# A rounded bias-table product, joined value products and a row factor moved behind a projection, in a hybrid RG-LRU and dilated-attention layer

## The chip, the cores and the metric

The kernel runs on one core of one Trainium2 chip, in one launch. The metric is the device time of the launch in microseconds; the median of three runs is given. The core has a matrix engine (TensorE, PE in the profile), a vector engine (VectorE, DVE), an activation engine (ScalarE, ACT), a general engine (GpSimd, POOL), and a queue engine (SyncE, SP) that only issues transfers. SP, ACT and POOL can each issue transfers between device memory and the on-chip memory. Each engine runs its own instructions in order and waits for the others by semaphores.

## What is computed

One layer of a bidirectional encoder on a sequence of 512 positions with 1024 channels, in 32-bit floats, as in this reference (cut):

```python
h = rms_norm(x, attn_norm_g)
xr, gate, q, k, v = split(h @ w_in)                 # 512 channels each
xr = centred_depthwise_conv(xr, conv_w, conv_b)
y_rnn = (rg_lru(xr, fwd) + rg_lru(xr, bwd)) * gelu(gate)
y_attn = dilated_attention(q, k, v, rel_bias)       # 8 heads of 64
mix = concat([rms_norm(y_rnn, norm_rnn_g), rms_norm(y_attn, norm_attn_g)])
x = x + mix @ w_out
h = rms_norm(x, mlp_norm_g)
x = x + square(relu(h @ w_up)) @ w_down             # 4096 hidden channels
return rms_norm(x, final_norm_g)
```

The attention of a head takes three windows of keys (strides 1, 4 and 16) with a bias that depends on the distance of key and query alone: `rel_bias` has 32 buckets by 8 heads. The kernel folds the three windows into one softmax over all 512 keys by adding to each score one number for the head and the distance: the bucket's bias, plus the logarithm of how many windows hold that distance, or -1e30 where none does. That table has 8 rows (heads) and 1024 columns (distances).

## The kernel before

Most tensors lie with channels on the 128 partitions and the 512 positions along the free dimension. Matrix products keep nearly full precision by splitting both operands into a rounded part (type fp32r, "hi") and the rounded remainder ("lo") and adding three rounded products (`mm3`, L222). Weights come from device memory as 128x1024 chunks on SP's queue (`emit_dma`, L182); each is split by ACT (`conv_hi`, L189) and DVE (`conv_lo`, L195) three chunks ahead of its use.

The order on each engine is the order of the program text: loops call small closures, and `plan` (L849) lists by hand which closure stands beside which step.

- The start (up to some 62 us) computes the recurrent input `pxr`, its convolution, the gates of the recurrence (`lru_gate`) and the value projection `pv`, 32 steps `n` of three rounded products (L592). In it `gate_weights` (L365) has POOL make the low parts of the gate weights, and `softplus_consts` (L120) has POOL make a few 128x8 constants, the last of them `chalf`.
- The bias table: ACT's queue loads `relt` (33 rows by 8: the 32 buckets and a row of ones) and two halves `oht` (33 rows by 512: a one-hot row for each bucket, and the logarithms) at L339 to L342. At step n = 18, `bias_prep` (L345) multiplies them on PE as plain 32-bit floats, DVE negates the result (`nbs`), and ACT's queue writes it to device memory (`nbd`). SP then loads, for each head, a 128x896 tile `tw` whose rows are shifted views of that row (`load_tw`).
- The gate projection and the first query and key projections follow (to some 100 us).
- The attention loop (L873) has 5 rounds `i` of 4 steps `u`. In round i, pair i of heads has its scores taken (`att_s`), reduced by DVE and exponentiated by ACT (`att_e`); pair i-1 has its probabilities transposed (`att_t`: PE to the two "et" buffers, and ACT copies them to `ett`). The value products of pair p (`att_av`, L742) run in two groups: key blocks 0 and 1 at step 2 of round p+1, key blocks 2 and 3 at step 0 of round p+2 (for the last pair after the loop). Each product writes 64 of the 128 rows of `pav`, two heads side by side. Beside each step run four "fillers": first the query and key projections of later pairs, then (`wo_thunks`, L780) the products of the recurrent half of `w_out`.
- The recurrent output `yrnn` (4 tiles) needs its RMS factor, one number for each position: squares (`sq_`, `add`), column sums on PE and the power on POOL (`rnn_cols`), then a tile with the factor along the free dimension on all partitions (`rnn_rows`: PE into an "et" buffer, and an ACT copy to `rr[0]`). DVE multiplies each `yrnn` tile by it (`rnn_scaled`, L506), and then the tile is split into hi (ACT, with the gain) and lo (DVE) for the products. The product of each of 8 output tiles is added to the residual `x1` by DVE (L792).
- After 210 us come the attention half of `w_out` and the feed-forward part, a dense stream of products to the end.

Of the kernel before, what the change touches and what calls it, by code (L numbers as in the profile page):

```python
# [12 lines left out]
FT = mybir.dt.float32  # L13
# [4 lines left out]
P = 128  # L18
# [22 lines left out]
for _n, _w in (("ag", 8), ("w0", 4), ("w1", 4), ("w2", 4), ("w3", 4), ("cb", 4),  # L41
# [2 lines left out]
    VEC[_n] = _o  # L44
    _o += _w
NVEC = _o


def bias_onehot():
    rel = np.arange(-(S - 1), S)  # L50
    m = np.zeros(rel.shape, np.int64)
    for window, dil in PATTERNS:
        half = window // (2 * dil)
        m += (rel % dil == 0) & (np.abs(rel) <= half * dil)
    nb = NBUCK // 2
    me = nb // 2
    n = np.abs(rel)
    nf = np.maximum(n, 1).astype(np.float32)
    large = me + (np.log(nf / np.float32(me)) / np.float32(math.log(MAXD / me))
                  * np.float32(nb - me)).astype(np.int32)  # L60
    large = np.minimum(large, nb - 1)
    bucket = np.where(rel > 0, nb, 0) + np.where(n < me, n, large)
    oh = np.zeros((NBUCK + 1, 2 * S), np.float32)
    oh[NBUCK, :] = NEG
    idx = np.arange(rel.size)
    keep = m > 0
    oh[bucket[keep], idx[keep]] = 1.0
    oh[NBUCK, idx[keep]] = np.log(m[keep].astype(np.float64)).astype(np.float32)
    return oh


@with_exitstack
def hybrid_kernel(ctx: ExitStack, tc, xw, xT, w_in, w_v, w_out, w_up, w_dn, gates, vecs, rel, onehot, fg, out):
# [261 lines left out]
            mm3(pxr[t], wk(t, k), hk(k), False, k == KD - 1)  # L335


    relt = consts.tile([NBUCK + 1, NH], FT, name="relt")
    nc.scalar.dma_start(relt, rel)  # L339
    oht = [work.tile([NBUCK + 1, S], FT, name="oht", tag="g", bufs=NG) for _ in range(2)]  # L340
    for i in range(2):
        nc.scalar.dma_start(oht[i], onehot[:, i * S:(i + 1) * S])  # L342
    nbd = dram.tile([NH, 2 * S], FT, name="nbd")

    def bias_prep():  # L345
        for i in range(2):
            pbz = ps_("pbias", "pj")
            nc.tensor.matmul(pbz[0:NH, :], lhsT=relt, rhs=oht[i], start=True, stop=True)
            nbs = g_("nbs", shape=(NH, S))
            nc.vector.tensor_scalar(nbs, pbz[0:NH, :], -1.0, None, op0=OP.mult)  # L350
            nc.scalar.dma_start(nbd[:, i * S:(i + 1) * S], nbs)
# [135 lines left out]
    def y_hi(k, y):  # L487
        ycat[k] = (g_("yh", FR), g_("yl", FR))
        act(ycat[k][0], y, AF.Copy, scale=vec("yg", k))

    def y_lo(k, y):
        hi, lo = ycat[k]
        stt(lo, y, vec("yg", k), f(hi), op0=OP.mult, op1=OP.subtract)
# [9 lines left out]
    def rnn_rows():  # L503
        rr[0] = row_tile(rc[0], "et")

    def rnn_scaled(*ts):  # L506
        for t in ts:
            nc.vector.tensor_tensor(yrnn[t], yrnn[t], rr[0], op=OP.mult)

    def rnn_split(*ts):  # L510
        for t in ts:
            y_hi(t, yrnn[t])
        for t in ts:
            y_lo(t, yrnn.pop(t))

    def proj_thunks(c, tag, done):
        o = {}

# [25 lines left out]
    def xmm(ks):  # L544
        for k in ks:
            mm3(pxr[3], wk(3, k), hk(k), k == 0, k == KD - 1)
# [11 lines left out]
    gate_weights(2)  # L558
    gate_weights(3)
    cneg, chalf = next(spc)  # L560
    xmm((1, 2, 3, 4))
    conv_b(0)
    conv_h(0)
# [28 lines left out]
    for n, (k, tt) in enumerate(steps):  # L592
        c = C_V + k // 2
        if k == 0:
            pv[tt] = ps_("pv", vtag[tt])
        hi, lo = splits[c]
        sl = slice((k % 2) * S, (k % 2 + 1) * S)
        tsl = slice(tt * P, (tt + 1) * P)
        mm3(pv[tt], (h_hi[:, k, tsl], h_lo[:, k, tsl]), (hi[:, sl], lo[:, sl]), k == 0, k == KD - 1)
        if n >= 16:  # L600
            feed(c, n % 8)
        if n in (8, 11, 14):
            conv_hi({8: 6, 11: 7, 14: 8}[n])
        if n in (9, 12, 15):
            conv_lo({9: 6, 12: 7, 15: 8}[n])
        if n >= GA and n < GA + 12 and (n - GA) % 3:
            t, m = (n - GA) // 3, 2 * ((n - GA) % 3 - 1)
            lru_gate(t, m)
            lru_gate(t, m + 1)
        if n == 0:  # L610
            conv_b(2)
        if n == 2:
            conv_b(3)
        if n == GA + 1:
            conv_h(2)
            conv_c(2)
        if n == GA + 2:
            conv_h(3)
            conv_c(3)
        lru_hooks(n)  # L620
        if n == 18:
            bias_prep()
            load_tw(0)
            load_tw(1)
# [155 lines left out]
    def wo_thunks(half, c2):  # L780
        c = C_WO + half * 4 + c2
        o = {}

        def mk(j, k):
            def run():
                if k == 0:
                    o["p"] = ps_("pwo", "pj")
                mm3(o["p"], wok(c, j, k), ycat[half * 4 + k], k == 0, k == 3)
                feed_q(c, 4 * j + k)
                if k == 3:  # L790
                    cc = 2 * c2 + j
                    nc.vector.tensor_tensor(x1[cc], x1[cc], o["p"], op=OP.add)  # L792
            return run
        return [mk(j, k) for j in range(2) for k in range(4)]

# [31 lines left out]
    def rnn_sq(t):  # L827
        y_sq(yrnn[t], 0)

    def scaled(t):  # L830
        return lambda: rnn_scaled(t)

    def hi(t):
        return lambda: y_hi(t, yrnn[t])

# [3 lines left out]
    def end(t):  # L839
        return lambda: rnn_end(t)  # L840

    def sq_(t):
        return lambda: rnn_sq(t)

    def add():
# [3 lines left out]
    plan = {(0, 0, 2): [sq_(0), add], (0, 0, 3): [end(1)],  # L849
            (0, 1, 1): [sq_(1)],  # L850
            (0, 2, 3): [add],
            (1, 0, 2): [end(2)], (1, 0, 4): [sq_(2)],
            (1, 1, 0): [add], (1, 1, 2): [end(3)], (1, 1, 4): [sq_(3)],
            (1, 2, 0): [add], (1, 2, 2): [rnn_cols], (1, 3, 1): [rnn_rows],
            (1, 3, 3): [scaled(0)], (1, 3, 4): [scaled(1), hi(0), hi(1)],
            (2, 1, 2): [lo(0), lo(1)], (2, 1, 3): [scaled(2), scaled(3), hi(2), hi(3)], (2, 2, 2): [lo(2), lo(3)]}
    for i in range(3):
        for key, (is_k, fn, e) in {(0, 2): (1, s_hi, 0), (0, 3): (1, s_hi, 1), (1, 0): (1, s_lo, 0), (1, 1): (1, s_lo, 1),
                                   (2, 2): (0, s_hi, 0), (2, 3): (0, s_hi, 1), (3, 0): (0, s_lo, 0), (3, 1): (0, s_lo, 1)}.items():
# [13 lines left out]
    for i in range(5):  # L873
        for u in range(4):
            if i < 4:
                att_s(i, u)
                if u == 0 and i < 3:
                    load_tw(2 * i + 2)
                if u == 2 and i < 3:
                    load_tw(2 * i + 3)  # L880
            if i >= 1:
                att_t(2 * i - 2, u)
                att_t(2 * i - 1, u)
            if i < 4:
                att_e(i, u)
            if u == 2 and i >= 1:
                att_av(i - 1, (0, 1))
            if u == 0 and i >= 1:
                att_z(i - 1)
            if u == 0 and i >= 2:  # L890
                att_av(i - 2, (2, 3))
            beside(i, u, 0)
            fill(1)
            beside(i, u, 1)
            fill(1)
            if u == 1 and i >= 1:
                att_r(i - 1)
            if u == 0 and i >= 2:
                att_y(i - 2)
            beside(i, u, 2)  # L900
            fill(1)
            beside(i, u, 3)
            fill(1)
            beside(i, u, 4)
# [25 lines left out]
    wo_b(0, 0)  # L930
    wo_b(0, 1)
    conv_hi(c + 3)
    att_av(3, (2, 3))
    att_y(3)
    wo_b(0, 2)
    for k in range(3):
# [353 lines left out]
```

## Time and profile before

| | us |
|---|---|
| runs (three) | 566.73, 566.97, 567.18; median 566.97 |
| profiled execution: its own time | 566.53 |
| profiled execution: span of the instructions | 564.8 |
| granted TensorE clock, mean over the span | 0.994 |
| busy: DVE, ACT, POOL | 388.7, 313.5, 51.9 |
| first bias product, first `nbs` | 53.3, 54.3 |
| attention loop, first and last step's transposes | 117.8, 198.5 |
| last matrix product starts | 555.3 |

"Span" is the time from the first to the last instruction of the profiled execution; its own time is longer by what lies around it. In the timeline view of the profile a row gives start and duration in us, engine, source line, operation, output <- inputs, the shape, how many instructions were merged (x8), and in brackets how long the engine had been idle and what ended that. A matrix product's duration includes its way through the array, and the next one starts earlier: the distance of two starts is what a product costs. A product of plain 32-bit floats shows as two rows.

### The profile page before, as it was taken

What the parts mean: (1) busy time and instruction counts of PE and PEld (TensorE: products, weight loads), DVE (VectorE), ACT (ScalarE), POOL (GpSimd) and SP (SyncE); (2) the same over time, 40 slices, a digit from 0 to 9 for tenths busy, and PEclk for the clock granted to TensorE, in tenths of its full rate; (3) what the DMA queues carried; (4) which work ended last, traced back from release to release, by engine and by line L of the source; (5) the groups of instructions that cost most, each with busy time, mean ns of one, the idle gap of its engine ahead of it and who ended that gap; (6) DMA issues with size and microseconds to landing.
All of it is one profiled execution on the core that took longest, in us unless ns stands there. A gap on an engine that the chain in (4) does not pass through costs nothing.

```text
span 564.8 us, 6888 instructions
## 1 busy us (share of the span) xinstructions
PE 554.5 (98%) x2520; PEld 445.0 (79%) x2520; DVE 388.7 (69%) x610; ACT 313.5 (56%) x510; POOL 51.9 (9%) x70
## 2 busy tenths in 40 slices
PE   9999999999999999999999999999999999999993
PEld 7887888677677678888888888888888888888782
DVE  6896499986774439453477778977233676896894
ACT  7669993686966434154463566553223243665654
POOL 3370000000000000000003033001000000131000
PEclk9999999999999999999999999999999999999997
DMA  7803434343351212242339799959623234699603
GB/s 262 297 12 113 169 113 149 113 131 113 111 187 38 74 38 75 75 149 75 104 109 287 171 268 275 266 164 258 186 84 104 77 110 98 194 252 262 163 1 149
DMA packets 25494, 82.97 MB, mean 147 GB/s; under 512 B 3106, under 2 KB 3234, under 8 KB 25460
## 3 DMA queue, kind: packets, MB, share of 16 engines
q1 hardware_dynamic: 19968, 64.50, 33.3%
q0 software_dynamic: 4608, 16.78, 15.5%
q10 hardware_dynamic: 884, 1.25, 0.7%
q8 instruction: 20, 0.33, 0.2%
q14 instruction: 14, 0.11, 0.1%
HBM read 78.81 MB, written 2.13 MB: 143 GB/s over the span
## 4 chain that ended last, share of the span: by engine, by line
PE 88%; DVE 6%; DMA 2%; ACT 2%; issue 1%; ACTq 0%; DVEq 0%
PE pu L224 10%; PE pu L223 10%; PE pu L225 10%; PE pd L224 6%; PE pd L223 6%; PE pd L225 6%; PE pqk L223 3%; PE pwo L223 3%; PE pav L749 3%; PE pqk L225 3%; PE pwo L225 3%; PE pwo L224 3%; PE pqk L224 3%; PE pt L716 2%; DMA wraw<-in_w_dn_dram 2%; DVE wlo L199 2%
## 5 line engine op out<-in xcount | busy, mean ns | idle before, releaser
L199 DVE TENSOR_TENSOR wlo<-wraw,whi 128x1024 fp32r<-128x1024 f32 x81 | 98.8, 1221 | 38.3 <-ACT whi L192 38.2
L192 ACT ACTIVATE whi<-wraw 128x1024 fp32r<-128x1024 f32 x81 | 85.4, 1055 | 41.1 <-PE pd L225 15.7
L223 PE MATMUL pu<-h2h,whi 128*128 128x512 f32 x256 | 100.5, 392 | 0.0
L225 PE MATMUL pu<-h2h,wlo 128*128 128x512 f32 x256 | 99.8, 390 | 0.0
L224 PE MATMUL pu<-h2l,whi 128*128 128x512 f32 x256 | 99.7, 390 | 0.0
L224 PE MATMUL pd<-wlo,ah 128*128 128x512 f32 x192 | 74.9, 390 | 0.1
L225 PE MATMUL pd<-whi,al 128*128 128x512 f32 x192 | 74.8, 389 | 0.0
L223 PE MATMUL pd<-whi,ah 128*128 128x512 f32 x192 | 74.8, 389 | 0.0
L1013 ACT ACTIVATE a<-pu 128x512 f32<-128x512 f32 x32 | 19.0, 597 | 97.6 <-PE pu L225 97.6
L1014 DVE TENSOR_TENSOR a<-a 128x512 f32<-128x512 f32 x32 | 22.1, 692 | 65.5 <-ACT a L1013 65.5
L225 PEld LDWEIGHTS pu<-h2h,wlo 128*128 128x128 f32 x256 | 48.1, 188 | 10.1
L223 PEld LDWEIGHTS pu<-h2h,whi 128*128 128x128 f32 x256 | 48.1, 188 | 9.8
L224 PEld LDWEIGHTS pu<-h2l,whi 128*128 128x128 f32 x256 | 48.1, 188 | 9.7
L224 PEld LDWEIGHTS pd<-wlo,ah 128*128 128x128 f32 x192 | 36.1, 188 | 7.9 <-DVE wlo L199 0.5
L223 PEld LDWEIGHTS pd<-whi,ah 128*128 128x128 f32 x192 | 36.1, 188 | 7.5
L225 PEld LDWEIGHTS pd<-whi,al 128*128 128x128 f32 x192 | 36.1, 188 | 7.4
L192 ACT ACTIVATE whi<-ts 128x1024 fp32r<-128x1024 f32 x24 | 25.5, 1061 | 24.2 <-PE pd L225 16.5
L199 DVE TENSOR_TENSOR wlo<-ts,whi 128x1024 fp32r<-128x1024 f32 x24 | 29.3, 1222 | 8.8 <-ACT whi L192 8.5
L205 POOL DMA_DIRECT2D ts<-in_w_dn_dram x16 | 16.9, 1175 | 106.5 <-DVE wlo L199 106.5
L223 PE MATMUL pqk<-h_hi,whi 128*128 128x512 f32 x64 | 26.5, 414 | 0.0
L223 PE MATMUL pwo<-yh,whi 128*128 128x512 f32 x64 | 26.3, 412 | 0.0
L718 ACT ACTIVATE ett<-pt 128x512 f32<-128x512 f32 x32 | 17.3, 590 | 15.8 <-PE pt L716 15.8
(210 smaller groups left out, 1031.6 us busy)
## 6 DMA issues: line engine op xcount, KB each, us to landing
wraw<-in_w_up_dram SPq DMA_DIRECT2D x32, 512.0 KB, 3.3
wraw<-in_w_dn_dram SPq DMA_DIRECT2D x24, 512.0 KB, 6.6
ts<-in_w_dn_dram POOLq DMA_DIRECT2D x24, 512.0 KB, 12.0
wraw<-in_w_in_dram SPq DMA_DIRECT2D x13, 512.0 KB, 3.3
wraw<-in_w_out_dram SPq DMA_DIRECT2D x8, 512.0 KB, 3.3
ts<-in_w_dn_dram SPq DMA_DIRECT2D x8, 512.0 KB, 5.3
tw<-in_w_dn_dram SPq DMA_DIRECT2D x8, 512.0 KB, 6.8
tw<-in_w_dn_dram POOLq DMA_DIRECT2D x8, 512.0 KB, 11.5
```

The costliest lines, as they stand in the source:

```text
L192: act(hi, raws[i], AF.Copy)
L199: nc.vector.tensor_tensor(lo, r, f(splits[i][0]), op=OP.subtract)
L205: nc.gpsimd.dma_start(r, wblock(c[0], nxt[1], c[2]), accum_op=OP.add)
L223: nc.tensor.matmul(o, lhsT=a[0], rhs=b[0], start=bool(first), stop=False)
L224: nc.tensor.matmul(o, lhsT=a[0], rhs=b[1], start=False, stop=False)
L225: nc.tensor.matmul(o, lhsT=a[1], rhs=b[0], start=False, stop=bool(last))
L716: nc.tensor.transpose(pt[:, qt * P:(qt + 1) * P], en[h][qt][:, jt * P:(jt + 1) * P], ident)
L718: act(t, pt, AF.Copy)
L749: nc.tensor.matmul(pav[p][a, :], lhsT=vs[:, jt, h * DH:(h + 1) * DH], rhs=et.pop((h, jt)), start=jt == 0, stop=jt == 3)
L1013: act(r, p, AF.Relu)
L1014: nc.vector.tensor_tensor(r, r, r, op=OP.mult)
```

## The change

It has three parts.

1. The bias table. `bias_rows` repeats the bucket rows on the host: buckets, buckets again, the row of logarithms, 31 zero rows, and that row again: 97 rows. `relt` becomes 97x128 (the 8 heads padded with zeros to 128 columns) and the halves of `oht` 97x512. They are loaded by POOL's queue, after `chalf`, in place of ACT's at the start. New `bias_round`, at steps n = 14 and n = 16, has DVE round them to fp32r: the second copy of the bucket rows gets the remainder of the table, and the last row gets the remainder of the logarithms (its factor is one). `bias_prep` then does one rounded product for each half.
2. The value products of a pair run in one group of eight at the later of the two places.
3. The row factor of the recurrent output is not multiplied into `yrnn`; it is multiplied into each of the 8 outputs of the recurrent projection, before the sum with `x1`. `rnn_scaled` and `rnn_split` go, and `plan` moves the squares, splits, column sums and row tile to other steps.

```diff
+NB3 = 3 * NBUCK + 1
...
-    return oh
+    return bias_rows(oh)
+
+
+def bias_rows(a):
+    b, last = a[:NBUCK], a[NBUCK:]
+    return np.concatenate([b, b, last, np.zeros((NBUCK - 1, a.shape[1]), np.float32), last], axis=0)
...
-    relt = consts.tile([NBUCK + 1, NH], FT, name="relt")
-    nc.scalar.dma_start(relt, rel)
-    oht = [work.tile([NBUCK + 1, S], FT, name="oht", tag="g", bufs=NG) for _ in range(2)]
-    for i in range(2):
-        nc.scalar.dma_start(oht[i], onehot[:, i * S:(i + 1) * S])
+    relt = consts.tile([NB3, P], FT, name="relt")
+    oht = [work.tile([NB3, S], FT, name="oht", tag="g", bufs=NG) for _ in range(2)]
     nbd = dram.tile([NH, 2 * S], FT, name="nbd")
+
+    ohr = []
+    relr = consts.tile([NB3, P], FR, name="relr")
+
+    def bias_round(i):
+        if i == 0:
+            r = slice(NBUCK, 2 * NBUCK)
+            nc.vector.tensor_copy(relr, relt)
+            nc.vector.tensor_tensor(relr[r], relt[r], f(relr)[r], op=OP.subtract)
+        t = work.tile([NB3, S], FR, name="ohr", tag="g", bufs=NG)
+        ohr.append(t)
+        r = slice(3 * NBUCK, NB3)
+        nc.vector.tensor_copy(t, oht[i])
+        nc.vector.tensor_tensor(t[r], oht[i][r], f(t)[r], op=OP.subtract)
 
     def bias_prep():
         for i in range(2):
             pbz = ps_("pbias", "pj")
-            nc.tensor.matmul(pbz[0:NH, :], lhsT=relt, rhs=oht[i], start=True, stop=True)
+            nc.tensor.matmul(pbz, lhsT=relr, rhs=ohr[i], start=True, stop=True)
...
     cneg, chalf = next(spc)
+    nc.gpsimd.dma_start(relt, rel)
+    for i in range(2):
+        nc.gpsimd.dma_start(oht[i], onehot[:, i * S:(i + 1) * S])
...
+        if n in (14, 16):
+            bias_round((n - 14) // 2)
         if n == 18:
             bias_prep()
...
-                    nc.vector.tensor_tensor(x1[cc], x1[cc], o["p"], op=OP.add)
+                    t = g_("wot")
+                    nc.vector.tensor_tensor(t, o["p"], rr[0], op=OP.mult)
+                    nc.vector.tensor_tensor(x1[cc], x1[cc], t, op=OP.add)
...
-            (1, 0, 2): [end(2)], (1, 0, 4): [sq_(2)],
-            (1, 1, 0): [add], (1, 1, 2): [end(3)], (1, 1, 4): [sq_(3)],
-            (1, 2, 0): [add], (1, 2, 2): [rnn_cols], (1, 3, 1): [rnn_rows],
-            (1, 3, 3): [scaled(0)], (1, 3, 4): [scaled(1), hi(0), hi(1)],
-            (2, 1, 2): [lo(0), lo(1)], (2, 1, 3): [scaled(2), scaled(3), hi(2), hi(3)], (2, 2, 2): [lo(2), lo(3)]}
+            (1, 0, 2): [end(2)],
+            (1, 1, 0): [sq_(2)], (1, 1, 2): [end(3)], (1, 1, 4): [add],
+            (1, 3, 0): [sq_(3)], (1, 3, 2): [hi(0)], (1, 3, 3): [add, hi(1)], (2, 0, 2): [rnn_cols],
+            (2, 0, 0): [lo(0), lo(1)], (2, 0, 4): [hi(2)],
+            (2, 1, 1): [rnn_rows], (2, 1, 2): [hi(3)], (2, 1, 4): [lo(2)], (2, 2, 3): [lo(3)]}
...
-            if u == 2 and i >= 1:
-                att_av(i - 1, (0, 1))
             if u == 0 and i >= 1:
                 att_z(i - 1)
             if u == 0 and i >= 2:
-                att_av(i - 2, (2, 3))
+                att_av(i - 2, range(4))
...
-    att_av(3, (2, 3))
+    att_av(3, range(4))
```

A key of `plan` is (round, step, place within the step).

## The prediction

> **What bounds the kernel now.** I read the page's busy table first, then who waits on TensorE (the waits view of PE), then the timeline of PE around each place that the change touches, and last DVE, ACT and POOL at the same moments.
>
> ```profile
> PE 554.5 (98%) x2520; PEld 445.0 (79%) x2520; DVE 388.7 (69%) x610; ACT 313.5 (56%) x510; POOL 51.9 (9%) x70
> PE pwarm L118 <- DVE epsb L109: 1.0, 1, 1.0
> 180.00:200.00 20.00, 20.00 (x110) 14.60 (x109) 8.84 (x15) 9.37 (x18) 0.00 (x0) 1.00 0.18 53
> ```
>
> PE is busy 98% of the span, and the only wait of PE in the waits view is 1.0 us before the first warm-up product. The third line (a stage: PE, PEld, DVE, ACT, POOL busy, clock, DMA share, GB/s) shows the attention stage: PE 20.00 of 20, clock 1.00, DVE not half busy. So PE sets the time, and an edit counts by what it takes from PE's stream or by the wait it puts into it. Busy is not the price, since matmuls overlap; the step from one start to the next is.
>
> ```profile
> 52.51 0.39 PE L223 MATMUL pv<-whi,h_hi 128*128 128x512 f32 x1
> 52.74 0.39 PE L224 MATMUL pv<-wlo,h_hi 128*128 128x512 f32 x1
> ...
> 53.28 1.88 PE L348 MATMUL pbias<-oht,relt 33*8 33x512 f32 x4
> 55.09 0.50 PE L223 MATMUL pv<-whi,h_hi 128*128 128x512 f32 x1
> 55.43 0.40 PE L224 MATMUL pv<-wlo,h_hi 128*128 128x512 f32 x1
> ...
> 122.31 1.03 PE L716 MATMUL pt<-ident,e 128*128 128x128 f32 x8
> 123.11 0.48 PE L223 MATMUL pqk<-h_hi,whi 128*128 128x512 f32 x1
> 123.42 0.40 PE L224 MATMUL pqk<-h_lo,whi 128*128 128x512 f32 x1
> ...
> 127.31 1.04 PE L716 MATMUL pt<-ident,e 128*128 128x128 f32 x8
> 128.27 1.94 PE L749 MATMUL pav<-ett,vs 128*64 128x512 f32 x8
> 130.14 0.50 PE L223 MATMUL pqk<-h_hi,whi 128*128 128x512 f32 x1
> 130.48 0.40 PE L224 MATMUL pqk<-h_lo,whi 128*128 128x512 f32 x1
> ```
>
> The pv rows are rounded (fp32r) products of 512 columns: one a 0.227 us. The two plain f32 bias products run as four passes (x4). An attention-value group (pav) holds four plain products, two jt by two heads, also two passes each: x8.
>
> **Part 1, the bias table.** From 53.28 to the second pv start after it (55.43) are 2.15 us; a pv product alone would have taken 0.23 of it, so the group costs 1.92. Afterwards it is two rounded products of 97 rows to 128 columns, the width of their neighbours: 2 x 0.227 = 0.45. Gain 1.47 us of PE. If the rounded product ran in two passes as the plain one does (0.43 each), it would be 0.2: I take one pass, since every f32r product in the page has one row.
>
> What it adds stands on DVE and POOL, and decides whether PE waits.
>
> ```profile
> 45.42 1.23 DVE L199 TENSOR_TENSOR wlo<-wraw,whi 128x1024 fp32r<-128x1024 f32 x1 [2.02 <-ACT whi L192]
> 48.68 1.23 DVE L199 TENSOR_TENSOR wlo<-wraw,whi 128x1024 fp32r<-128x1024 f32 x1 [2.03 <-ACT whi L192]
> 49.83 3.70 DVE L407 TENSOR_TENSOR ga<-ga,xc 128x512 f32<-128x512 f32 x6
> 54.34 0.68 DVE L350 TENSOR_SCALAR nbs<-pbias 8x512 f32<-8x512 f32 x1 [0.82 <-PE pbias L348]
> 39.85 0.71 POOL L145 TENSOR_SCALAR chalf<-sp 128x8 f32<-128x8 f32 x1
> ```
>
> bias_round(0) stands on DVE between the first two lines: table copy and difference (128 columns, some 0.2 us each, an estimate from the 0.36 of the 128x384 cast at L256), one 97x512 copy (0.43, the row of the 512-column copy L729) and a one-row difference (0.69, as any 512-column two-input row): 1.4 us in an idle 2.03, free. bias_round(1) stands behind four of the six L407 (0.60 apart): 49.83 + 2.41 = 52.24, then 0.36 + 0.69 and about 0.06 for the signal: 53.35. PE's second product wants it at 53.28 + 0.23 = 53.51. No wait, with 0.16 us to spare. lru_x(2), nbs and lru_x(3) behind it come 1.1 us later; the weight difference after them (59.98) had been idle for 2.84 us, so nothing beyond it moves.
>
> This holds if the rows have landed. Three issues leave ACT, where they hid beside a wait for weights (2.49 us idle before 19.62): worth nothing to PE. They stand on POOL behind chalf, which ends at 40.56; nothing of POOL's waits behind them until the rnn factor some 90 us later. Two POOL issues in a row start 0.55 to 0.92 us apart in the trace, so the halves are issued at about 41.2 to 41.5 and 41.8 to 42.4. If the first half lands at t, PE waits until t + 5.7 (0.36 + 0.69 copy and difference, 1.15 weight difference, 2.41 for L407, 0.36 + 0.69, signal 0.06) against 53.51: a landing up to 47.8 is free, then each us costs a us.
>
> ```profile
> ts<-in_w_dn_dram POOLq DMA_DIRECT2D x24, 512.0 KB, 12.0
> DMA to landing us min/median/max: 5.3/14.0/19.4
> q10 hardware_dynamic: 44, 0.07, 8.6%
> ```
>
> No plain load from POOL is in the trace: all 32 of its transfers add 512 KB into a tile (first two lines; the least, 5.3 us, is a lone one). Those packets are 4 KB and take 0.327 us, eight to each DMA engine: 2.6 us, so 2.7 us of a lone one is start and completion. A half of the table is 97 rows of 2 KB; on the ACT queue such a row took 0.084 us (the packet records of the old load). Over 16 engines it is 7 rows: 0.6 us, landing 3.3 us after issue, at 44.7; with the 5.3 of the nearest row, 46.7. Both are free. Upper bound: all 97 rows on one engine, 97 x 0.084 = 8.1, landing at 41.4 + 2.7 + 8.1 = 52.2, a wait of 4.4 us (on one and the same engine the second half would come at 60.3: 7.9 us); or the median of all, 12.0, at 53.4: 5.6. The third line (17 to 21 us: packets, MB, share) is one old load of 33 rows: 44 packets, 33 rows and 11 more, one for each engine: it went to 11 engines with three rows each, not to 16. I take 3.3 to 5.3, because the cost above the transfer is nearest to a lone POOL row.
>
> By the Trainium skill, DMA: Bandwidth & Descriptors, section "Why a DMA increments its semaphore by 16 and not by 1", a copy takes the largest number of engines up to 16 that divides its rows, which is 11 for 33 rows: the trace agrees. By that rule 97, a prime, would take one engine, and the sum would be a loss; the same section has an exception for some copies from GpSimd, with the rows rounded up over 16, and by that the sum stays. No run here yet shows which. [...]
>
> **Part 2, value products in one group.** From pt at 127.31 to the second pqk at 130.48 are 3.17 us; the same stretch without the group (122.31 to 123.42) is 1.11. A group costs 2.06: four pairs of passes 0.43 apart (1.72) and 0.34 of entering and leaving the 64-column products. A joined group is 8 x 0.43 + 0.34 = 3.78 against 4.12. The last pair's second group (200.87) stands alone and joins too, so four pairs gain 4 x 0.34 = 1.38 us. If the entry were paid anew inside, nothing: the three equal steps in each group speak against that. The transposed tiles wait a step longer for their reader; there are 48 buffers of that tag, and about 25 are taken between.
>
> **Part 3, the row factor.** PE's work is the same: column sums (0.90) and row tile (0.44) only move, the first from step (1,2) to (2,0), the second from (1,3) to (2,1). DVE loses four products at 138 to 151 us (0.68 each) and gains eight at 160 to 200 (0.69 each, before each sum). Cover: DVE is idle 8.1 and 11.2 us in the two stages 160 to 180 and 180 to 200, and 5.5 is asked. Queued behind each pwo sum are the next step's score reductions, which PE's next scores wait for; without cover, eight times up to 0.69. The shortest step without value products is 0.80 + 12 x 0.227 + 0.09 + 0.91 = 4.5 us; DVE's in it 1.3 (reductions) + 0.6 (half a weight difference) + 1.3 + about 0.7 = 3.9. It fits. One thing gets late: the row tile now goes into the "et" buffer that the first transposes of its step leave.
>
> ```profile
> 146.45 1.04 PE L716 MATMUL pt<-ident,e 128*128 128x128 f32 x8
> 147.38 1.06 ACT L718 ACTIVATE ett<-pt 128x512 f32<-128x512 f32 x2
> ```
>
> In the old place the row tile came 1.56 us after pt; here that is 148.01, while the first ett copy, behind a weight cast, ends at 147.97 and needs its signal. I put 0.1 us (0 to 0.5, the second copy).
>
> **Sum.** 1.47 + 1.38 - 0.1 = 2.75 us. The profiled execution took 566.53 us (span 564.8, and 1.7 around it): 563.8. The median of the runs is 0.44 above it, so 566.97 - 2.75 = 564.2. After 210 us every stage is PE's dense stream, so the gain passes through: 10 us of PE idle lie at the start and behind the last product, and neither is touched.
>
> **Rivals.** (a) The rows come late, slower than before. Place: PE's bias products. Price: a us for each us that the first half lands after 47.8; at a landing of 50.5 the gain is gone, from 51.7 on the kernel is slower. One engine: 564.2 + 4.4 = 568.6; 12.0 us: 569.8. For it: 33 rows took 11 engines, a divisor, and 97 has none up to 16 but 1; and every POOL transfer is between 5.3 and 19.4. Against: those moved 2.6 times the bytes, adding, with DMA engines up to 90% busy; here their share is 0.25. Chance 0.12. (b) Late by part of that, landing at 48 to 50.5: 564.5 to 567. POOL's small rows at 31 to 40 us take 0.7 instead of 0.2 beside busy DVE, which speaks for some delay. 0.10. (c) The attention stage gives a part back: steps without value products shrink from 6.6 to 4.5 us while ACT, 16.4 of 20 us busy at 140 to 160, has as much to do; three pairs losing up to 0.5 each: 565.7. Against: the time taken there comes back in the joined step (9.2 us). 0.09. (d) Rounded product in two passes, or entry paid again: 565.0 to 565.6. 0.03.
>
> **How the numbers follow.** Forecast 0.66 (563.7 to 564.6). I call 0.2%, 1.1 us, what can be told from no change: faster is under 565.8, slower over 568.1. Faster: forecast, nearly all of (c), (d), half of (b): 0.66 + 0.08 + 0.03 + 0.05 = 0.82, less 0.04 for what I don't see: 0.78. Same: rest of (b) and (c) and a little: 0.10. Slower 0.12. The range reaches from 563.6 through (c) to the end of (b), 566.8.
>
> **What would show it.** In the changed profile: two pbias rows 0.23 apart and no wait of PE for DVE ahead of them (wait there: rival a or b, with the landing of oht to match); four pav rows of x16, each 3.35 to the last start; the row tile 1.6 us behind its transposes; DVE idle still left between 160 and 200 us; one lag of 2.7 us from 210 to the end. Wrong it would be if PE shows any wait of more than 0.5 us.

## The result and the profile after

The changed kernel took 564.01 us (median of six executions, the fastest 563.5; five lie within 564.71), the kernel before 567.0 us in the same comparison: a ratio of 0.9947, 95% interval 0.9933 to 0.9961. Run again for the study it took 564.53 us against 566.88 us, ratio 0.9951 (0.9937 to 0.9965). One of the first six executions, the one that was profiled, took 1,984.56 us with its products 0.84 us apart, which no other execution did; the profile shown here is that of the second time (e0_after, 564.53 us, span 562.8 us).

First its busy table:

```profile
PE 552.2 (98%) x2518; PEld 445.5 (79%) x2518; DVE 394.7 (70%) x620; ACT 313.4 (56%) x510; POOL 54.0 (10%) x73
```

Then what PE waited for (us in total, times, longest):

```profile
PE pwarm L124 <- DVE epsb L115: 1.0, 1, 1.0
PE pd L230 <- DVE wlo L205: 0.7, 1, 0.7
```

And the stage 180 to 200 us (columns as in the prediction):

```profile
180.00:200.00 20.00, 20.00 (x109) 13.04 (x107) 9.91 (x15) 8.35 (x15) 0.00 (x0) 1.00 0.16 53
```

PE is still the bound. The wait of 0.7 us lies at 529 us, far from the change: a product starts 0.87 us later there than the usual distance of two products (0.227 us). The same product is late by 0.26 us in the kernel before, and by anything from nothing (e4_late_rows) to 0.72 us (e6_value_cols) in the other profiles. DVE has 10.1 us of idle time left in the last attention stage (11.2 before).

Then PE's timeline around the bias products, an attention step without value products, one with them, and the new place of the row tile:

```profile
53.29 0.39 PE L231 MATMUL pv<-whi,h_lo 128*128 128x512 f32 x1
53.52 0.79 PE L366 MATMUL pbias<-ohr,relr 97*128 97x512 f32 x2
54.15 0.40 PE L229 MATMUL pv<-whi,h_hi 128*128 128x512 f32 x1
...
130.80 1.04 PE L729 MATMUL pt<-ident,e 128*128 128x128 f32 x8
131.59 0.48 PE L229 MATMUL pqk<-h_hi,whi 128*128 128x512 f32 x1
...
135.34 1.04 PE L729 MATMUL pt<-ident,e 128*128 128x128 f32 x8
136.31 3.65 PE L762 MATMUL pav<-ett,vs 128*64 128x512 f32 x16
139.89 0.50 PE L229 MATMUL pqk<-h_hi,whi 128*128 128x512 f32 x1
...
145.94 0.40 PE L231 MATMUL pqk<-h_hi,wlo 128*128 128x512 f32 x1
146.27 0.62 PE L308 MATMUL prow<-ident,rcol 128*128 128x128 f32 x4
```

The bias group is two rows (x2) and 0.63 us long, from 53.52 to 54.15; the second of the two starts at 53.83. A joined value group is sixteen rows and 3.58 us long where two groups took 1.87 each; the transposes before it last 0.97 us to the next start, where those without a group last 0.79. The row tile follows the product before it by 0.33 us, 0.1 more than the distance of two products.

Last the rows of the table on their way. POOL's issues:

```profile
40.92 0.84 POOL L569 DMA_DIRECT2D relt<-in_rel_dram  x1
41.76 1.13 POOL L571 DMA_DIRECT2D oht<-in_onehot_dram  x2
```

The page's line for the transfer (KB each, us from issue to landing):

```profile
oht<-in_onehot_dram POOLq DMA_DIRECT2D x2, 194.0 KB, 2.9
```

And DVE:

```profile
47.44 0.43 DVE L360 CAST ohr<-oht 97x512 fp32r<-97x512 f32 x1
47.90 0.69 DVE L361 TENSOR_TENSOR ohr<-oht,ohr 1x512 fp32r<-1x512 f32 x1
48.99 1.23 DVE L205 TENSOR_TENSOR wlo<-wraw,whi 128x1024 fp32r<-128x1024 f32 x1 [0.40 <-ACT whi L198]
...
52.54 0.42 DVE L360 CAST ohr<-oht 97x512 fp32r<-97x512 f32 x1
53.00 0.69 DVE L361 TENSOR_TENSOR ohr<-oht,ohr 1x512 fp32r<-1x512 f32 x1
```

The first half landed at 41.76 + 2.9 = 44.7 us. Its rounding stands in an idle stretch of DVE. The second half's ends at 53.69, and PE's second bias product starts at 53.83, 0.147 us later and 0.316 us after the first. That product waits for DVE. In every run with the changed table it starts 0.146 or 0.147 us after this rounding ends, while its distance from the first product varies from 0.316 (here) to 0.44 us (e5_rows_act_queue); and the two products of e4_late_rows that wait for DVE for far longer start 0.146 us after the rounding too. Against the usual distance the wait is 0.09 us here; the waits view doesn't list it, since the products overlap.

The parts are worth a quarter of a per cent each, and single executions of the kernel before spread over 0.3% (566.32 to 568.13 us), so the parts are also read by lag: the start of the same product in two profiles, subtracted. The change of the lag from one landmark to the next belongs to the stage between them. (Start of the product in the profile, less that in the kernel before; us.)

| | last input product, 28.8 | last gate product, 50.9 | first gate projection, 64.1 | last projection product, 224.6 | last product, 555.3 |
|---|---|---|---|---|---|
| e0_after | +0.41 | +0.33 | -1.06 | -2.29 | -1.69 |
| e1_bias_alone | +0.34 | +0.22 | -1.13 | -1.26 | -1.22 |
| e2_value_alone | +0.42 | +0.06 | +0.06 | -0.37 | -0.14 |
| e3_row_alone | +0.13 | -0.23 | -0.23 | -0.13 | -0.11 |
| e6_value_cols | +0.55 | +0.19 | +0.19 | -1.17 | -0.68 |
| e11_no_factor_move | +0.27 | +0.17 | -1.18 | -2.53 | -2.32 |
| e9_pairs_joined | +0.70 | +0.62 | -0.77 | -2.54 | -2.52 |
| e10_cols_rounded | -0.83 | -0.88 | -2.23 | -4.93 | -4.68 |

From the last gate product to the first gate projection is the bias stage, from there to the last projection product are attention and projections. In these two stages, a kernel whose products there are those of the kernel before differs from it by up to 0.13 us (e1_bias_alone in the attention stage). The other stages are alike in all these kernels and still differ, so they are not read: the start (first column) by the clock and the inputs, see the last section; from there to the last gate product by 0.05 to 0.36 us, most of it at one gate product at 38 us; and behind 224.6 us by up to 0.60 us, at the product at 529 us named above.

### The profile page after: what moved, and what is told of

It is laid out like the page before. It is cut to its first block, busy times and chain, and to the rows that moved or that the text cites. A ratio compares the mean times of both kernels' runs of the same rounds, so it can differ in the third digit from the quotient of the medians.

```text
span 1982.7 us, 6892 instructions
## 1 busy us (share of the span) xinstructions
PE 1974.8 (100%) x2518; PEld 1018.1 (51%) x2518; DVE 402.6 (20%) x620; ACT 319.5 (16%) x510; POOL 51.0 (3%) x73
## 4 chain that ended last, share of the span: by engine, by line
PE 100%; DVE 0%; ACT 0%; issue 0%
PE pu L230 11%; PE pu L229 11%; PE pu L231 11%; PE pd L229 9%; PE pd L230 9%; PE pd L231 9%; PE pqk L229 3%; PE pwo L229 3%; PE pwo L230 3%; PE pqk L230 3%; PE pqk L231 3%; PE pav L762 3%; PE pwo L231 3%; PE pt L729 3%; PE pv L229 1%; PE pp L229 1%
## 5 line engine op out<-in xcount | busy, mean ns | idle before, releaser
L229 PE MATMUL pu<-h2h,whi 128*128 128x512 f32 x256 | 283.1, 1106 | 0.0
L230 PE MATMUL pu<-h2l,whi 128*128 128x512 f32 x256 | 281.3, 1099 | 0.0
L231 PE MATMUL pu<-h2h,wlo 128*128 128x512 f32 x256 | 279.1, 1090 | 0.0
L229 PE MATMUL pd<-whi,ah 128*128 128x512 f32 x192 | 211.0, 1099 | 0.0
L230 PE MATMUL pd<-wlo,ah 128*128 128x512 f32 x192 | 210.7, 1097 | 0.0
L231 PE MATMUL pd<-whi,al 128*128 128x512 f32 x192 | 208.1, 1084 | 0.0
L231 PE MATMUL pwo<-yh,wlo 128*128 128x512 f32 x64 | 70.1, 1095 | 0.0
L230 PE MATMUL pwo<-yl,whi 128*128 128x512 f32 x64 | 69.8, 1090 | 0.0
L231 PE MATMUL pqk<-h_hi,wlo 128*128 128x512 f32 x64 | 69.8, 1090 | 0.0
L230 PE MATMUL pqk<-h_lo,whi 128*128 128x512 f32 x64 | 69.6, 1088 | 0.0
```

The lines of the kernel that those rows point to most:

```text
L229: nc.tensor.matmul(o, lhsT=a[0], rhs=b[0], start=bool(first), stop=False)
L230: nc.tensor.matmul(o, lhsT=a[0], rhs=b[1], start=False, stop=False)
L231: nc.tensor.matmul(o, lhsT=a[1], rhs=b[0], start=False, stop=bool(last))
```

## Experiments: the parts

e0_after is the changed kernel as it is.

> The changed kernel once more, for a profile beside those of its parts. Additive theory: 2.75 us under the kernel before; two pbias rows 0.23 us apart in PE's timeline, four pav rows of x16, no wait of PE above 0.5 us. Rival (rows of the table late, partly): a wait of PE for DVE ahead of the bias products, and the gain is under 2.3 us.

Ratio 0.9951, 2.35 us under the kernel before, with no more than the 0.09 us of wait at the second bias product. In the attention stage it gained 2.29 - 1.06 = 1.23 us, in the bias stage 0.33 + 1.06 = 1.39.

e1_bias_alone applies the table's part of the diff to the kernel before:

```diff
+NB3 = 3 * NBUCK + 1
...
-    nc.scalar.dma_start(relt, rel)
...
+    nc.gpsimd.dma_start(relt, rel)
...
+        if n in (14, 16):
+            bias_round((n - 14) // 2)
```

> The kernel before with the bias table alone changed. Additive theory: 1.47 us under the kernel before (0.26%, about 565.5), all of it at 53 to 56 us, and none given back behind it. Rival 1 (rows late): less than 1.2 us, with a wait of PE ahead of the bias products. Rival 2 (the gain of the whole comes from the value products or the row factor, and the bias group is hidden by a stall later): under 0.4 us.

Measured 564.83 us, ratio 0.9966 (0.9955 to 0.9976), 1.4 to 2.6 us by the interval; in the lag 1.35 us, all of it at 51 to 56 us, and nothing given back behind.

e2_value_alone joins the value products in the kernel before:

```diff
-            if u == 2 and i >= 1:
-                att_av(i - 1, (0, 1))
...
-                att_av(i - 2, (2, 3))
+                att_av(i - 2, range(4))
...
-    att_av(3, (2, 3))
+    att_av(3, range(4))
```

> The kernel before with the value products alone joined. Additive theory: 1.38 us under the kernel before (0.24%, about 565.6), 0.34 us at each of four pairs. Rival (the shorter steps without value products wait for ACT or DVE, which the row factor's moved work would have relieved): 0 to 0.9 us, with a wait of PE for ACT in the steps that lost their group.

Measured 566.61 us, ratio 0.9994 (0.9985 to 1.0003), 0.43 us in the lag. The rival was right about the sum. A single wait took it, in PE's timeline:

```profile
129.38 0.39 PE L225 MATMUL pqk<-h_hi,wlo 128*128 128x512 f32 x1
130.52 1.02 PE L322 MATMUL pcs<-ones,ysq 128*128 128x1 f32 x8 [0.75 <-DVE ysq L483]
```

And DVE at the same time:

```profile
129.68 0.69 DVE L483 TENSOR_TENSOR ysq<-ysq 128x512 f32<-128x512 f32 x1
```

The column sums of the recurrent output start 1.14 us after the product before them, 0.9 more than the usual distance (0.23). They wait for a sum of squares that DVE ends at 130.37. It ended at 130.31 in the kernel before too, but there a value group of 1.9 us stood ahead of the column sums, which came at 131.65. The joined group moved to the next step and uncovered it.

e3_row_alone applies the third part alone, plan and all:

```diff
-                    nc.vector.tensor_tensor(x1[cc], x1[cc], o["p"], op=OP.add)
+                    t = g_("wot")
+                    nc.vector.tensor_tensor(t, o["p"], rr[0], op=OP.mult)
+                    nc.vector.tensor_tensor(x1[cc], x1[cc], t, op=OP.add)
...
-            (1, 2, 0): [add], (1, 2, 2): [rnn_cols], (1, 3, 1): [rnn_rows],
...
+            (1, 3, 0): [sq_(3)], (1, 3, 2): [hi(0)], (1, 3, 3): [add, hi(1)], (2, 0, 2): [rnn_cols],
```

> The kernel before with the row factor alone moved behind the projection. Additive theory: within 0.3 us of the kernel before (PE's products are the same, 0 to 0.5 us of a wait at the row tile). Rival 1 (DVE's eight extra products lie on the way to the next scores): up to 5.5 us slower, 0.69 us in each step that waits. Rival 2 (PE did wait for the old DVE products somewhere): 0.5 to 1 us faster.

Measured 566.9 us, ratio 1.0 (0.9991 to 1.0009), 0.10 us of loss in the attention stage, at the row tile: it starts 0.33 us after the product before it, and 0.15 us after the first `ett` copy ends, as in e0_after. Neither rival.

e6_value_cols is e2_value_alone with two entries of the plan moved:

```diff
-            (1, 2, 0): [add], (1, 2, 2): [rnn_cols], (1, 3, 1): [rnn_rows],
+            (1, 2, 0): [add], (1, 2, 4): [rnn_cols], (1, 3, 2): [rnn_rows],
```

> The kernel before with the value products joined, as in e2_value_alone, and only the recurrent column sums moved two places on (step (1,2), place 4) and their row tile one place (step (1,3), place 2); the row factor stays where it was. Theory (the joined group's gain was given back by PE waiting 0.88 us at these column sums for DVE's sum of squares): no wait at them, 1.36 us under the kernel before. Rival (the joined group gains nothing without the row factor's move, since DVE's work of the old place delays the shorter steps): within 0.6 us of the kernel before, with another wait of PE.

Measured 565.63 us, ratio 0.9977 (0.9968 to 0.9986), and 0.19 + 1.17 = 1.36 us in the lag. PE's row has no wait any more:

```profile
131.14 0.95 PE L322 MATMUL pcs<-ones,ysq 128*128 128x1 f32 x8
```

So the joined groups are worth what was forecast, 0.34 us each, only if the column sums come later. In the changed kernel the third part's plan moves them to step (2,0).

e11_no_factor_move asks whether the row factor had to move at all: bias table and e6_value_cols together, `rnn_scaled` left as it was.

> The kernel before with the bias table and the value products changed, the column sums and row tile moved as in e6_value_cols, and the row factor left on the recurrent output. Theory (the factor's move gains nothing and costs 0.13 us at the row tile): 2.8 us under the kernel before, the time of the changed kernel or 0.1 less. Rival (with the gates' end earlier, the recurrent products or splits come late for their readers without the factor's move): 0.5 us or more over the changed kernel, with a wait of PE at 125 to 165 us.

Measured 563.4 us, ratio 0.9936 (0.9923 to 0.995); in the lag 1.35 in each of the two stages, against 1.39 and 1.23 of the changed kernel. The factor's move brought nothing that two moved entries don't, and its 0.1 us at the row tile is saved. By the times alone this kernel and the changed one can't be told apart.

## Experiments: the bias table

e7_plain_padded keeps plain products and pads the table to 128 columns:

```diff
-    relt = consts.tile([NBUCK + 1, NH], FT, name="relt")
+    relt = consts.tile([NBUCK + 1, P], FT, name="relt")
...
-            nc.tensor.matmul(pbz[0:NH, :], lhsT=relt, rhs=oht[i], start=True, stop=True)
+            nc.tensor.matmul(pbz, lhsT=relt, rhs=oht[i], start=True, stop=True)
```

> The kernel before with its bias table padded to 128 columns; products still plain f32, two of four rows in all. Theory (passes cost, not the width of the output): four rows 0.43 apart remain, at most 0.3 us of entering and leaving goes: 0 to 0.3 us under the kernel before. Rival (the narrow output of 8 columns is what costs, and rounding is not needed): two rows 0.23 to 0.3 apart, 1 us or more under the kernel before.

Measured 566.65 us, ratio 0.9998 (0.9989 to 1.0007):

```profile
52.83 1.98 PE L348 MATMUL pbias<-oht,relt 33*128 33x512 f32 x4
54.74 0.50 PE L223 MATMUL pv<-whi,h_hi 128*128 128x512 f32 x1
```

Four rows, 1.91 us to the next start, as with 8 columns (1.81). The passes cost, not the width.

e4_late_rows holds the loads back on POOL, by a copy of one element that must wait for a weight cast of ACT:

```diff
-    nc.gpsimd.dma_start(relt, rel)
-    for i in range(2):
-        nc.gpsimd.dma_start(oht[i], onehot[:, i * S:(i + 1) * S])
...
+    def late_rows():
+        nc.gpsimd.tensor_copy(late, f(splits[8][0])[0:1, 0:1])
+        nc.gpsimd.dma_start(relt, rel)
+        for i in range(2):
+            nc.gpsimd.dma_start(oht[i], onehot[:, i * S:(i + 1) * S])
...
+        if n == 14:
+            late_rows()
```

> The changed kernel, its three row loads held on POOL until ACT's weight cast that began at 47.85 in its profile has ended (48.96): issues at about 49.2, 50.1, 50.6, the first half lands 2.9 us after its issue, at 53.0. Theory (a landing up to 47.8 is free, then each us costs a us, and nothing gives it back): a wait of 5.2 us on PE before the bias products, 569.4. Rival 1 (work queued behind catches up later, since DVE and ACT have slack): under 3 us over the changed kernel. Rival 2 (the weight differences behind the blocked DVE queue make it worse): over 7 us.

Measured 571.46 us, ratio 1.0083 (1.007 to 1.0097), 6.9 to 7.5 us over the two medians of the changed kernel, and 7.3 by the lag against e0_after. PE's timeline, and DVE's second rounding:

```profile
54.16 0.39 PE L231 MATMUL pv<-whi,h_lo 128*128 128x512 f32 x1
54.97 0.47 PE L374 MATMUL pbias<-ohr,relr 97*128 97x512 f32 x1 [0.43 <-DVE ohr L369]
59.70 0.77 PE L374 MATMUL pbias<-ohr,relr 97*128 97x512 f32 x1 [4.26 <-DVE ohr L369]
60.26 0.63 PE L229 MATMUL pv<-whi,h_hi 128*128 128x512 f32 x1
60.69 0.63 PE L230 MATMUL pv<-wlo,h_hi 128*128 128x512 f32 x1
...
58.86 0.69 DVE L369 TENSOR_TENSOR ohr<-oht,ohr 1x512 fp32r<-1x512 f32 x1
```

Two stretches behind the wait (the granted clock is third from the end):

```profile
62.00:64.50 2.50, 2.50 (x7) 1.97 (x6) 2.50 (x5) 2.09 (x3) 0.00 (x0) 0.50 0.07 13
64.50:66.00 1.50, 1.50 (x7) 1.24 (x6) 1.43 (x3) 1.50 (x4) 0.00 (x0) 0.92 0.40 98
```

Over the distances in e0_after, the waits are 0.59 and 4.41 us, 5.0 in all, close to the theory's 5.2 (the half landed at 53.7, and PE itself came 0.9 us later). The other 2.3 us are the clock: behind the wait it was granted at 0.50, and until 64.6 us the products came 0.43 us apart instead of 0.23. None of the three theories had this; rival 2 had the number for another reason. By the Trainium skill, TensorE: Matmul & The Clock Gate, in its Part 1 on the clock gate, PE falls to half clock after an idle window of about 3.4 us and needs about as long of work to come back; the traces agree in part. Their clock records have half clock from 57.9 to 64.7 us here and from 58.3 to 61.7 us in the next run: it came back 5.0 and 3.1 us after the products resumed, but it fell 2.5 us into PE's idle time here and 3.9 us into it there.

e8_rows_less_late has the same edit with the weight cast before (`splits[7]`, n == 11).

> As e4_late_rows, but POOL holds the loads only until the weight cast before (the one that began at 44.63 and ended at 45.70): issues of the halves at about 46.7 and 47.3, landing of the first at 49.5, so a wait of PE of 1.7 us in all, by the 5.9 us from landing to the second product that e4_late_rows showed. Theory 1 (the loss of 2.3 us at half clock behind the wait of e4_late_rows comes only behind a wait of some microseconds; the 1.6 us step at 22.89 in e5_rows_act_queue had none): 1.7 us over the changed kernel, 565.9, clock 1.00 behind the wait. Theory 2 (any wait there costs the clock): products 0.43 apart behind it, 3 to 4 us over the changed kernel, 567 to 568.

Measured 570.8 us, ratio 1.0073 (1.0059 to 1.0087): 6.3 to 6.8 us over the changed kernel where 1.7 or 3 to 4 was expected. POOL's copy:

```profile
45.66 1.23 POOL L352 COPY late<-whi 1x1 f32<-1x1 f32 x1 [4.91 <-ACT whi L198]
```

DVE:

```profile
45.63 1.23 DVE L205 TENSOR_TENSOR wlo<-wraw,whi 128x1024 fp32r<-128x1024 f32 x1 [2.03 <-ACT whi L198]
52.04 0.23 DVE L363 CAST relr<-relt 97x128 fp32r<-97x128 f32 x1 [5.19 <-DMA relt<-in_rel_dram]
```

And the page's line for the table's transfer:

```profile
relt<-in_rel_dram POOLq DMA_DIRECT2D x1, 48.5 KB, 5.2
```

The loads came late twice over. POOL's copy of one element took 1.23 us, exactly as long as DVE's subtraction beside it (0.18 us in e4_late_rows, with DVE idle). By the Trainium skill, SBUF — State Buffer, section "SBUF: two separate sides", DVE with two inputs in SBUF and a GpSimd operation that reads SBUF need the same port, which one of them holds for its whole instruction; the trace agrees. Then the table took 5.2 us to land instead of 2.5: in the packet records a weight load of 512 KB from SP's queue runs from 47.8 to 50.0, and the table's packets only from 49.3 to 49.9. Of its sixteen completion signals fifteen came by 50.4 us and the last at 52.0; what held that one back is not shown. So PE waited 0.42 and 4.41 us, and the clock fell again, at a cost of 1.4 us. The run doesn't tell the two theories apart: of how long a wait costs the clock, the runs show only that the 1.6 us step of the next experiment does not, that 4.4 us do, twice, and that the clock had fallen 2.5 us into one of these. What e8_rows_less_late shows beside that is how narrow the place of the loads is in the changed kernel: they land in 2.9 us with no large load beside them, their last packets at 44.7, and the next weight load's begin at 44.8.

e5_rows_act_queue puts the three loads back on ACT's queue, where the kernel before has them:

```diff
-    nc.gpsimd.dma_start(relt, rel)
-    for i in range(2):
-        nc.gpsimd.dma_start(oht[i], onehot[:, i * S:(i + 1) * S])
...
+    nc.scalar.dma_start(relt, rel)
...
+        nc.scalar.dma_start(oht[i], onehot[:, i * S:(i + 1) * S])
```

> The changed kernel with the three row loads on ACT's queue, at their place in the kernel before. Theory 1 (on ACT's queue 97 rows, a prime, go to one DMA engine, row after row): each half takes 97 x 0.084 = 8.1 us on one engine and lands 10 to 20 us after its issue, still before 47.8, so the time is that of the changed kernel within 0.5 us: which queue fetches the rows is worth nothing here. Theory 2 (spread over the engines as on POOL's queue): landing 3 us after issue, the same time. Rival (three issues on ACT or the crowded engine delay the first weights): 1 us or more over the changed kernel.

Measured 567.67 us, ratio 1.0018 (1.0009 to 1.0027): 3.1 to 3.7 us over the changed kernel, the whole gain gone. ACT's timeline, and in the last row the two issues of the kernel before:

```profile
18.20 5.11 ACTq L348 DMA_DIRECT2D oht<-in_onehot_dram  x2
23.36 2.95 ACT L198 ACTIVATE whi<-wraw 128x1024 fp32r<-128x1024 f32 x3 [6.04 <-issue]
...
16.55 3.02 ACTq L342 DMA_DIRECT2D oht<-in_onehot_dram  x2
```

PE's:

```profile
22.89 0.40 PE L231 MATMUL pxr<-h_hi,w3l 128*128 128x512 f32 x1
24.47 0.50 PE L229 MATMUL pxr<-h_hi,whi 128*128 128x512 f32 x1 [1.19 <-ACT whi L198]
25.73 0.50 PE L231 MATMUL pxr<-h_hi,wlo 128*128 128x512 f32 x1 [0.53 <-DVE wlo L205]
```

And ACT's DMA queue at 39 to 44 us (packets, MB, share of 16 engines):

```profile
q10 hardware_dynamic: 61, 0.12, 6.5%
```

Theory 1 was right about the engine: 61 rows in 5 us, one after another, are 6.5% of sixteen engines, that is one. It was wrong that this costs nothing. The last row's packet ended at 44.2 us, early enough, but ACT was held from the first issue at 18.20 to the end of the second at 23.32 us, its first weight cast began at 23.36 instead of 17.45 us (e0_after), and PE waited: the lag against the kernel before is 2.27 us at 28.8 us and 3.38 at 50.9. Two things held ACT. Each issue starts 0.02 us after the last completion signal of a weight load whose semaphore its own load takes (signals at 18.18 and 20.81 us); the kernel before waits the same way (16.53 and 19.25 us), and its first cast began at 19.62. And the second issue itself lasted 2.49 us, where each of the two of 33 rows lasted 0.3 us. Why the first of 97 rows lasted only 0.24 us, and whether the rows on that one engine delayed the weight load's signal at 18.18 (the other fifteen had come by 16.55), no run shows. The step of 1.58 us from 22.89 to 24.47 left the clock alone: the products behind it are 0.23 us apart again.

## Experiments: beyond the change

e9_pairs_joined adds three edits to the changed kernel (and puts the `wo_b` steps behind the loop into another order, which the diff below does not show):

```diff
-NB3 = 3 * NBUCK + 1
+NB3 = 128
...
-            (2, 1, 1): [rnn_rows], (2, 1, 2): [hi(3)], (2, 1, 4): [lo(2)], (2, 2, 3): [lo(3)]}
+            (2, 1, 2): [rnn_rows, hi(3)], (2, 1, 4): [lo(2)], (2, 2, 3): [lo(3)]}
...
-    att_av(3, range(4))
-    att_y(3)
+    for p in (2, 3):
+        att_av(p, range(4))
+        att_y(p)
```

> The changed kernel with three edits: the value products of the last two pairs in one group of sixteen after the loop; the row tile of the recurrent factor one place later; the table of the biases padded from 97 to 128 rows. Theory: one entry of 0.34 us less, 0.13 us of the row tile's wait less, and 0.18 us less if the 0.31 instead of 0.23 us between rounded bias products comes from their 97 rows: 0.5 to 0.65 us under the changed kernel. Rival (the products of the third pair had covered something in the last round, or the projection behind them now waits for the third pair's scaling): a wait of PE after 195 us, and no gain.

Measured 563.2 us, ratio 0.9941 (0.9928 to 0.9953); in the attention stage 1.77 us of lag against 1.23: 0.54 more, the 0.34 and 0.13 forecast and a little. The group of both pairs:

```profile
193.19 7.09 PE L762 MATMUL pav<-ett,vs 128*64 128x512 f32 x32
200.21 0.50 PE L229 MATMUL pwo<-yh,whi 128*128 128x512 f32 x1
```

It takes 7.02 us where two took 3.58 each. The padding brought nothing: the rounded bias products stand 0.34 and 0.31 us apart as with 97 rows, so the time above their neighbours' distance doesn't come from the rows. In the first distance it is the wait for DVE; the 0.08 us in the second, between the second bias product and the next `pv` product, stay open.

e10_cols_rounded carries the bias table's idea to the column sums of the two outputs:

```diff
+            nc.tensor.matmul(pc[:, 2 * tt:2 * tt + 2], lhsT=ss[:, tt * P:(tt + 1) * P], rhs=onesr, start=True, stop=True)
...
-        pend[half] = g_("ysq")
+        pend[half] = g_("ysq", FR)
```

> e9_pairs_joined, and the column sums of the squares of the recurrent and of the attention output by one rounded product each instead of a plain one (the squares and their sums are rounded). Theory (a plain product of one column pays its passes as the bias products did: eight rows, 0.96 us a group): four rows, 0.4 to 0.5 us a group, two groups: 0.9 to 1.1 us under e9_pairs_joined. Rival (the loads of the 128x128 squares set the pace, whatever the passes): 0 to 0.3 us.

Measured 562.64 us, ratio 0.9926 (0.9914 to 0.9939), the fastest kernel of the study; its interval and that of the changed kernel just overlap. In the lag the attention stage gains 2.70 us, 0.93 more than e9_pairs_joined, as forecast. First the group in e0_after, then in e10_cols_rounded:

```profile
141.38 0.95 PE L328 MATMUL pcs<-ones,ysq 128*128 128x1 f32 x8
142.19 0.49 PE L229 MATMUL pqk<-h_hi,whi 128*128 128x512 f32 x1
```

```profile
140.18 0.50 PE L336 MATMUL pcs<-onesr,ysq 128*128 128x2 f32 x4
140.54 0.47 PE L229 MATMUL pqk<-h_hi,whi 128*128 128x512 f32 x1
```

Half the rows, 0.36 us instead of 0.81 to the next start.

## Why the prediction was right, and where its steps were not

The time forecast, 564.2 us, lies between the two medians. By its steps:

- **Bias products: 1.47 us forecast, 1.35 to 1.39 measured.** The mechanism held (one pass, e7_plain_padded), two sizes were off: the rounded products cost 0.31 us each, not 0.227, and the old group cost 2.02 us, not 1.92, since I had left out that the first row came 0.32 us after the product ahead of it. That the two nearly cancel is luck.
- **Landing of the rows: at 44.7 us forecast, 44.7 measured.** The lower of the two values that I took was right; the packet records show the table in thirteen packets of seven rows and one of six. So of the two rules of the Trainium skill, DMA: Bandwidth & Descriptors, section "Why a DMA increments its semaphore by 16 and not by 1", the exception with the rows rounded up over 16 holds for POOL's queue (7 rows each), and the divisor rule for ACT's (e5_rows_act_queue, one engine). The delay beside busy DVE that rival (b) reckoned with did not show: POOL issued the loads at 40.92 to 42.88 us with DVE at work for most of it, and the table's packets run from 42.46, while DVE is at a weight difference (42.48 to 43.71).
- **The spare time at the second rounding: 0.16 us forecast, a wait of 0.09 us measured.** "No wait" failed here, by a little: the forecast took 0.36 us for the copy (0.42 measured; at the first rounding it had taken 0.43 itself) and 0.06 us for the signal, where the product starts 0.147 us after the rounding ends. In e1_bias_alone and e11_no_factor_move the wait is 0.13 us.
- **"Three issues leave ACT ... worth nothing to PE" was the wrong question.** It holds for the old 33 rows, though ACT's 2.49 us of idle time were not a wait that the issues hid beside: the second issue made it, since the first cast behind it had its weights at 16.53 us. For 97 rows the change of queue is worth 3.2 us (e5_rows_act_queue, by the lag at 224.6 us).
- **Price of late rows, "then each us costs a us": wrong in size.** The wait was as forecast (5.0 us), but a wait of 4.4 us in one piece cost another 1.4 to 2.3 us of clock, and rival (a) would have been dearer by that.
- **Value products: 1.38 us forecast, 1.36 measured** in e6_value_cols, for the reason given (0.18 us of leaving the transposes and 0.16 of entering each group).
- **"Column sums (0.90) and row tile (0.44) only move": the step that failed.** The move of the column sums was put at nothing. Their move is what lets the value products keep their gain: without it, 0.9 us are lost at the column sums. Rival (c) saw such a loss coming, but from ACT; it was DVE's sum of squares. As the change moves the column sums, the sum came out right for a reason that the parts, as I priced them, do not show; so far as the working goes, that was luck.
- **Row tile: 0.1 us forecast, 0.10 to 0.13 measured.** The cause is the one forecast: it starts 0.15 us after the first `ett` copy ends. DVE's eight extra products were hidden, as forecast.
- **The sign of being wrong, "any wait of more than 0.5 us".** As written it came up: the 0.7 us at 529 us, which cost the profiled execution 0.61 us more than the kernel before loses at the same product. The wait is for a weight difference of DVE, far behind all three parts, and in the other profiles it does not grow with the gain (0.27 us late in e9_pairs_joined, 0.72 in e6_value_cols). That speaks against the change as its cause; what sets it was not tested.

## What to carry to other kernels

A plain 32-bit product pays for its passes however small it is: small helper products in a stream of rounded ones are worth counting. When work leaves a step, look at what stood behind it there; a wait that it covered may take the gain, and moving the waiting instruction by a place or two gives it back. How soon a small load lands depends on the queue that it is given and on whether a large load runs beside it, and a load that made the matrix engine wait 4.4 us cost more than the wait.

## What the runs showed of the hardware that was not expected

- **The clock after a wait.** 4.41 us of wait cost 2.3 us more at half clock in e4_late_rows and 1.4 in e8_rows_less_late; a 1.58 us step cost none.
- **The same start takes a different time in each execution.** At the last input product, 28.8 us, the lag against the kernel before lies between -0.83 (e10_cols_rounded) and +1.33 us (e4_late_rows), though PE's products are the same in both up to there. First e4_late_rows, then e10_cols_rounded, the same six products:

```profile
4.69 1.62 PE L338 MATMUL pxr<-h_hi,w3h 128*128 128x512 f32 x3
6.11 1.14 PE L338 MATMUL pxr<-h_lo,w3h 128*128 128x512 f32 x3
```

```profile
4.67 0.93 PE L346 MATMUL pxr<-h_hi,w3h 128*128 128x512 f32 x3
5.44 0.93 PE L346 MATMUL pxr<-h_lo,w3h 128*128 128x512 f32 x3
```

Three products take 1.42 us to the next start in the one and 0.77 in the other: the clock came up later. The stage view's granted clock reads 1.00 at 4 to 7 us in both, but that is no measurement: the clock records in the traces begin only at 6.7 us in e4_late_rows and at 4.7 us in e10_cols_rounded, with full clock, and from about there on the products come 0.23 us apart. The clock is not all of it: in e7_plain_padded the records begin at 6.7 us too, and its lag at 28.8 us is -0.09; in e4_late_rows PE's products also stand still for 1.14 us from 7.54 us, in e10_cols_rounded they don't. This is part of why single executions differ by half a microsecond and more, and why the stages were compared by lag.
- **Issuing can block.** An issue of a load of 97 rows on ACT's queue lasted 2.49 us (the second of two in e5_rows_act_queue), where those of 33 rows in the kernel before lasted 0.3 us. And from 16.84 to 19.27 us in the kernel before, ACT's second issue waited for a weight load that uses the same semaphore, with a cast behind it whose own weights had landed.
